# Two SwiGLU layers on one core: first gate and up products held in PSUM around the last norm, VectorE's order there written out, and the stream split for the projections out of SBUF

## The chip, the core and the metric

The kernel runs on one core of a Trainium2 chip. The core has a matrix engine (TensorE, PE in the rows), VectorE (DVE), ScalarE (ACT), GpSimd (POOL) and a queue engine (SyncE, SP) that issues most of the transfers between device memory and the on-chip memory SBUF. Matrix products are summed in PSUM, which the kernel uses as eight banks. The metric is the device time of one execution in microseconds (us); lower is better.

## What is computed

One inference step of a two-layer trunk on 1088 tokens (1024 of a prompt, 64 of eight sampled sequences) of width 1024. Layer 0 mixes by causal trailing means, layer 1 by dilated window attention; after each mixer comes a SwiGLU block, and between the layers one key/value and one query projection are made of the residual stream:

```python
def _rmsnorm(x, g):
    xf = x.astype(F32)
    y = xf * lax.rsqrt(jnp.mean(xf * xf, axis=-1, keepdims=True) + EPS)
    return (y * g.astype(F32)).astype(x.dtype)

def _swiglu(h, w_gate, w_up, w_down):
    return (jax.nn.silu(h @ w_gate) * (h @ w_up)) @ w_down
...
# layer 0:  x += PoolMix(RMSNorm(x));       x += SwiGLU(RMSNorm(x))
# then:     kv = RMSNorm(x) @ w_kv          (keys: per-head norm and rotary)
# layer 1:  x += DilatedAttn(RMSNorm(x));   x += SwiGLU(RMSNorm(x))
```

## The kernel before

**Precision.** Every f32 operand of a product is split in a high and a low part (`split`, L198 on ScalarE makes the high part, L199 on VectorE the low one), and every product is three matmuls (`mm3`, L202 to L204). A weight tile is split just before it is used.

**Layout.** The residual stream is `xall`, 128 partitions by 8 feature chunks by 1088 tokens. The tokens are handled as four quarters of 272 (`NB`), q0 to q3, or, for the projections, as nine tiles of 128 (the last of 64) in the order `TORD` = 5, 6, 7, 8, 0, ..., 4.

**SwiGLU.** Gate and up are computed by a scheme of seven block products for two-by-two blocks. The left factors are blocks of the weight or sums of them (`STEPS`: A11, A12, S2, S3, S1, A22, S4; the sums are made on VectorE, L423 to L428), the right factors are blocks or sums of the normed stream (`MATE`: B11, B21, T2, T3, T1, T4, B22), one tile of 128x1088 for each half g = 0, 1. B11 and B21 need quarters q0 and q1 only (`forms_one`). The five others need q2 and q3 too (`forms_two`, L269 to L279): half 0 needs q0 and q2, half 1 needs q1 and q3. All five are made from `xall` in place, so `xall` ends as scratch and its memory is given back; the stream itself has been stored to device memory (`spill`) and is loaded again for the down product. A unit of gate_up is 128 columns of the gate or the up weight: seven products for two halves of 12 matmuls each (168 matmuls). The output of the first product of a unit is copied out of PSUM by ScalarE into a tile `u` (L488); the tiles `u` lie in memory that `xall` held.

**The norm** of a quarter (`Norm.finish`): sums of squares over features by matmuls with a column of ones (L243), reciprocal square root on VectorE (L190 to L195), a transposition that spreads it over the partitions (L252), a copy on ScalarE (L254), and eight multiplications on VectorE (L257).

**Start of gate_up.** `EARLY = 2` gate/up pairs, four units, load their A11 and A12 blocks ahead (`load_early`) and run the products with B11 and B21 first, 192 matmuls, before the first product that needs a T form. Each engine executes its own instructions in order; where no manual order is set, a scheduler chooses that order when the program is built (before, GpSimd's order alone is manual in this part).

**Down.** `Down.run` goes through the steps A11, S1, S2, S4, S3, A12, A22, the first six over both halves (eight banks, 264 matmuls each), the last one half at a time. After S3 the quarters q2 and q3 of the stream are finished: VectorE adds the bank to a tile `du` (L630), GpSimd adds that twice into the stream (L631, L632), sixteen additions. `after(q)` is called when quarter q is done: it stores the quarter (layer 0) or writes output (layer 1). The weights of down come in tiles of 512 KB through a small pool of buffers.

**After down of layer 0** `split_stream` loads the nine tiles of the stream from device memory into `skt`, splits them into yh and yl, squares them on ScalarE, sums the squares per token (L721), and makes one matmul with ones per tile; from these sums comes the norm that the projections apply at their end. The weights of the projections are scaled by the norm's gain and split on ScalarE (L778) and VectorE (L779).

**PSUM** is divided by names: in gate_up and down all eight banks are "f" (`STR_PS`), elsewhere `FFN_PS` and `ATT_PS`.

## Time and profile before

| what | value |
|---|---|
| median of 3 runs | 3232.81 us (3223.08 to 3241.59) |
| the profiled execution | 3224.75 us |
| its span, first to last instruction | 3223.0 us |
| TensorE busy | 3056.5 us, 95% of the span |
| mean granted TensorE clock | 0.965 of full speed |
| layer 0: mixer; norm and forms; gate/up; down | to 136; to 180; to 632; to 881 us |
| projections; attention; output projection w_o | to 1790; to 2350; to 2458 us |
| layer 1: norm and forms; gate/up; down; last stores | to 2506; to 2955; to 3214; to 3223 us |

The busy share is a mean over stages. The stage borders are read from the timeline of the engines and are rounded. TensorE idles in a few places only, and nearly all of them lie where one stage ends and the next begins.

### The profile page before, as it was taken

The numbers are of one execution on the slowest core, as the hardware profiler recorded it, in microseconds if no ns is written. First come the engines' busy times: TensorE is split into PE (matmuls) and PEld (weight loads), VectorE is DVE, ScalarE is ACT, GpSimd is POOL, SyncE is SP. The second block draws the span as 40 slices with busy tenths as digits, with TensorE's granted clock in tenths as the row PEclk, the third lists the DMA queues.
The fourth block names the chain that finished last, engine by engine and source line by source line (L and its number), as shares of the span: only waits on it lengthen the run. The fifth ranks groups of instructions, "written<-read, shape, count | busy, mean of one in ns | idle before, by whom it ended". The sixth has DMA issues, their size and how long they took to land.

```text
span 3223.0 us, 56332 instructions
## 1 busy us (share of the span) xinstructions
PE 3056.5 (95%) x20467; PEld 2782.2 (86%) x20467; DVE 2315.0 (72%) x4669; ACT 1412.9 (44%) x4384; POOL 704.8 (22%) x829
## 2 busy tenths in 40 slices
PE   6599999999889999999999899999997899999998
PEld 6599999999877777777777788888897899999998
DVE  4676666667689999888893477777747666665675
ACT  4333322333466555243351577776723332232333
POOL 2313333255200000000000002222213233333551
PEclk8699999999999999999999799999998999999999
DMA  6336777788866776876965758686474267778876
GB/s 233 124 113 208 256 252 241 272 315 278 303 174 228 237 228 213 315 269 219 338 209 159 207 170 281 225 278 223 145 248 159 92 238 242 243 250 297 285 271 230
DMA packets 318106, 747.00 MB, mean 232 GB/s; under 512 B 38366, under 2 KB 140814, under 8 KB 315029
## 3 DMA queue, kind: packets, MB, share of 16 engines
q1 hardware_dynamic: 284103, 515.79, 49.3%
q0 software_dynamic: 5376, 174.60, 15.0%
q10 hardware_dynamic: 28350, 53.03, 4.5%
q8 instruction: 161, 2.64, 0.3%
q14 instruction: 116, 0.95, 0.1%
HBM read 629.57 MB, written 295.37 MB: 287 GB/s over the span
## 4 chain that ended last, share of the span: by engine, by line
PE 81%; DMA 7%; DVE 5%; issue 2%; POOL 2%; ACT 2%; SPq 0%; ACTq 0%; DVEq 0%; POOLq 0%
PE ps_f L202 12%; PE ps_f L204 12%; PE ps_f L203 12%; PE ps_s L1095 4%; PE ps_o L1128 4%; PE ps_s L202 3%; PE ps_s L203 3%; PE ps_s L204 3%; PE ps_a L202 2%; PE ps_a L204 2%; PE ps_a L203 2%; PE ps_p L203 2%; PE ps_p L202 2%; DMA wraw<-in_w_down 2%; PE ps_p L204 2%
## 5 line engine op out<-in xcount | busy, mean ns | idle before, releaser
L169 POOL DMA_DIRECT2D out_kv_sample<-in_cache_kv_w x168 | 83.8, 502 | 1466.1 <-PE ps_o L204 898.5
L202 PE MATMUL ps_f<-hf,wsplit 128*128 128x272 f32 x1232 | 342.4, 291 | 14.6 <-DVE du L630 5.5
L203 PE MATMUL ps_f<-hf,wsplit 128*128 128x272 f32 x1232 | 350.2, 289 | 0.5 <-DVE hf L199 0.5
L204 PE MATMUL ps_f<-hf,wsplit 128*128 128x272 f32 x1232 | 339.7, 290 | 6.2 <-DVE wsplit L199 6.2
L202 PEld LDWEIGHTS ps_f<-hf,wsplit 128*128 128x128 f32 x1232 | 229.9, 191 | 17.1 <-ACT wsplit L198 9.0
L199 DVE TENSOR_TENSOR wsplit<-wraw,wsplit 128x512 fp32r<-128x512 f32 (+1 forms) x250 | 189.1, 766 | 72.3 <-ACT wsplit L198 66.5
L198 ACT CAST wsplit<-wraw 128x512 fp32r<-128x512 f32 (+1 forms) x250 | 153.4, 633 | 196.8 <-DVE wsplit L199 76.4
L204 PEld LDWEIGHTS ps_f<-hf,wsplit 128*128 128x128 f32 x1232 | 228.0, 190 | 7.7 <-DVE wsplit L199 7.3
L203 PEld LDWEIGHTS ps_f<-hf,wsplit 128*128 128x128 f32 x1232 | 233.9, 190 | 0.7 <-DVE hf L199 0.7
L198 ACT CAST wsplit<-wsplit 128x512 fp32r<-128x512 f32 x176 | 108.6, 619 | 273.0 <-PE ps_f L204 272.2
L199 DVE TENSOR_TENSOR hf<-hraw,hf 128x544 fp32r<-128x544 f32 (+1 forms) x176 | 166.7, 955 | 83.6 <-ACT hf L198 83.5
L199 DVE TENSOR_TENSOR wsplit<-wsplit 128x512 fp32r<-128x512 f32 x176 | 155.0, 882 | 65.0 <-ACT wsplit L198 64.6
L198 ACT CAST hf<-hraw 128x544 fp32r<-128x544 f32 (+1 forms) x176 | 102.6, 590 | 174.6 <-PE ps_f L204 151.7
L1106 ACT ACTIVATE S<-S,ml 128x128 f32<-128x128 f32 (+1 forms) x384 | 169.1, 443 | 22.3 <-DVE ml L1101 21.7
L199 DVE TENSOR_TENSOR vl<-vc,vh 128x512 fp32r<-128x512 f32 x208 | 143.9, 715 | 47.6 <-ACT vh L198 46.9
L461 POOL TENSOR_TENSOR sg<-sg,ct 128x544 f32<-128x544 f32 x66 | 103.8, 1573 | 309.6 <-DVE ct L459 193.2
L747 DVE TENSOR_TENSOR spr<-skt,sqb 128x1024 f32<-128x1024 f32 x128 | 155.2, 1212 | 20.8 <-DMA sqb<-q 19.9
L748 DVE TENSOR_REDUCE sc<-spr 128x16 f32<-128x1024 f32 x128 | 154.4, 1206 | 1.0
L1128 PEld LDWEIGHTS ps_o<-wsplit,P 128*128 128x128 f32 x1120 | 143.7, 196 | 6.9 <-ACT U L1132 1.1
L1128 PE MATMUL ps_o<-wsplit,P 128*128 128x64 f32 x1120 | 148.0, 273 | 0.7 <-ACT U L1132 0.5
L198 ACT CAST vh<-vc 128x512 fp32r<-128x512 f32 x208 | 122.8, 617 | 58.6 <-DMA vc<-in_cache_kv_w 31.7
L1095 PE MATMUL ps_s<-akT,aqT 64*128 64x128 f32 x1120 | 142.5, 301 | 0.0
(439 smaller groups left out, 10254.5 us busy)
## 6 DMA issues: line engine op xcount, KB each, us to landing
sqb<-q SPq DMA_DIRECT2D x128, 512.0 KB
wraw<-in_w_down SPq DMA_DIRECT2D x104, 512.0 KB
vc<-in_cache_kv_w SPq DMA_DIRECT2D x208, 256.0 KB
skt<-in_cache_kv_w SPq DMA_DIRECT2D x96, 512.0 KB
wraw<-in_w_gate SPq DMA_DIRECT2D x48, 512.0 KB
wraw<-in_w_up SPq DMA_DIRECT2D x48, 512.0 KB
wraw<-in_w_kv SPq DMA_DIRECT2D x48, 512.0 KB
out_kv_sample<-in_cache_kv_w POOLq DMA_DIRECT2D x24, 960.0 KB, 7.1
```

Of the source, the lines that this page charges most:

```text
L169: c = bulk.dma_start(_raw(kv_s[b], (n * WIN[b] + r) * row, [[row, m], [1, row]]), _raw(caches[b], (n * WIN[b] + r + TS) * row, [[row, m], ...
L198: nc.scalar.copy(h, x)
L199: nc.vector.tensor_sub(l, x, h.bitcast(FT))
L202: nc.tensor.matmul(out, wh, xh, start=first, stop=False, **kw)
L203: nc.tensor.matmul(out, wh, xl, start=False, stop=False, **kw)
L204: mark[0] = nc.tensor.matmul(out, wl, xh, start=False, stop=last, **kw).ins
L461: nc.gpsimd.tensor_mul(s, s, t)
L747: nc.vector.tensor_mul(pr, kt, qb)
L748: nc.vector.tensor_reduce(sc[b][:, :, n * TS + t], pr.rearrange("p (h d) -> p h d", d=HD), axis=AX.X, op=OP.add)
L1095: nc.tensor.matmul(ps[hh][:, c:c + 128], self.qT[hs, jj, :], kt[hs, jj, :], start=True, stop=True)
L1106: nc.scalar.activation(subs[hh][:, e], subs[hh][:, e], AF.Exp, bias=self.ml[:, 0, h:h + 1], scale=-1.0, accum_out=self.ml[:, 1, h:h + 1])
L1128: nc.tensor.matmul(self.po[:, h % 8 * 64:h % 8 * 64 + 64], Ps[hh][:, c:c + 128], vv[:, h * 64:(h + 1) * 64], start=z == 0, stop=z == nb - 1)
```

## The change

It has four parts.

1. **Around the last norm of each layer.** One bank is taken from "f" and named "n" for the sums and the transposition of the last quarter's norm. Only two units are loaded ahead. Their eight products with B11 and B21 (12 matmuls each) are started with seven "f" banks and kept there; nothing is copied out until the forms are done (`drain`, L546). The sums of q3 stand ahead of the products, its transposition (`apply`) ahead of the eighth product, the forms behind it. VectorE's order is manual here; the forms are made half by half and form by form (`FORMS`: T2, B22, T1, T3, T4), with tiles of their own for each half.
2. **Layer 1.** w_o goes through the quarters as q0, q2, q1, q3 (`QORD`); the norms of q0, q2 and q1 run as `pending` pieces between the products of w_o, and the forms of half 0 are made there too.
3. **Stream split.** The tiles of the stream are split straight out of `xall`: tiles 5 to 8 inside down, when S3 has finished q2 and q3 (`after0`, with an "f" bank), tiles 0 to 4 at the start of the projections. The nine loads into `skt` go. The stores of x1 move from SyncE's queue to GpSimd's.
4. **Smaller.** The outputs of layer 1 are written in halves of 512 features, the first half of tiles 0 to 4 after A12; the scores of the sampled tokens multiply in place; the attention's output is split by quarters (`pieces`); gate_up has one copy group more.

```diff
-STR_PS = {"f": 8}
+STR_PS = {"f": 7, "n": 1}
+DOWN_PS = {"f": 8}
+QORD = (0, 2, 1, 3)
...
+            self.sums(q, tag)
+            self.apply(q, gain, tag)
+        def sums(self, q, tag):
...
+        def apply(self, q, gain, tag):
...
-    def forms_two(X):
...
+    def forms_sum(g):
+        y11, y12, y21, y22 = quarter(0, g), quarter(0, g + 2), quarter(1, g), quarter(1, g + 2)
+        nc.vector.tensor_sub(y12, y22, y12)
+        nc.vector.tensor_add(y11, y11, y12)
+        nc.gpsimd.tensor_sub(y21, y11, y21)
+
+    def forms_two(X, g, f):
+        y11, y12, y21, y22 = quarter(0, g), quarter(0, g + 2), quarter(1, g), quarter(1, g + 2)
+        split(*X[f, g], {"T2": y11, "T3": y12, "B22": y22, "T1": y22, "T4": y21}[f])
+        if f == "B22":
             nc.vector.tensor_sub(y22, y22, y11)
+    FORMS = ("T2", "B22", "T1", "T3", "T4")
...
-    EARLY = 2
...
-        for n in range(2 * EARLY):
-            load_early(n)
-        for j in range(7):
+        dve = tc.manual_schedule(engines={mybir.EngineType.DVE})
+        dve.__enter__()
+        load_early(0)
+        load_early(1)
+        step = iter(begin)
+        first = {}
+        def drain(n):
+            u = tiles(n)
+            for g in range(2):
+                nc.scalar.copy(u[:, g], first[n, "A11", g][:, :NB])
+            for g in range(2):
+                take(n, "B11", g, first[n, "A12", g][:, :NB], u[:, g], OP.add)
+        for n in range(2):
+            for f in ("A11", "A12"):
+                for g in range(2):
+                    if n and f == "A12" and g:
+                        for done in step:
+                            done()
+                        prep(0, "A11")
+                        pl = open_pool()
+                        drain(0)
+                    p = first[n, f, g] = bank("f")
+                    product(p, n, f, g, True, True)
+                    if n == 0 and f == "A11":
+                        next(step)()
+        drain(1)
+        dve.__exit__(None, None, None)
+        for j in range(1, 7):
             prep(0, STEPS[j])
-        for n in range(2 * EARLY):
-            one(n)
...
+    def begin(X, gain, norm, rest):
+        def sums():
+            norm.sums(3, "n")
+        def apply():
+            norm.apply(3, gain, "n")
+            forms_sum(1)
+        def forms():
+            for f in FORMS:
+                for g in rest:
+                    forms_two(X, g, f)
+        return sums, apply, forms
...
-            x = pl.tile([128, D], FT, name="skt", bufs=3).rearrange("p (k t) -> p k t", k=8)
-            for q in range(o // NB, (o + n - 1) // NB + 1):
-                lo, hi = max(o, q * NB), min(o + n, (q + 1) * NB)
-                sync.dma_start(x[:, :, lo - o:hi - o], x1[q][:, :, lo - q * NB:hi - q * NB])
+            x = xall[:, :, o:o + n]
...
+    def after0(q):
+        if q != "A12":
+            spill("x1", (q,), x1, bulk)
+        if q == 3:
+            split_stream(yp[0], TORD[:4], "f")
...
     def projections():
+        split_stream(y2, TORD[4:], "p")
...
-            split_stream(pl, TORD[:4])
             load(0)
-            split_stream(pl, TORD[4:])
...
-            for q in range(4):
+            for q in QORD:
...
+                        if m < 6 and pending:
+                            pending.pop(0)()
+                if m4:
                     spill("x2", (q,), x2)
-                    nq.finish(q, G_F1, "s")
-                    forms_one(X, q)
+                    if q < 3:
+                        pending += ending(q)
...
+    form_tiles_two(X, xb.enter_context(pool("xb1", side="left")))
+    forms_sum(0)
+    for f in FORMS:
+        forms_two(X, 0, f)
...
+    def after1(q):
+        if q == 3:
+            output((5, 6, 7, 8), 0)
+            output((5, 6, 7, 8), 1)
+        elif q == "A12":
+            output((0, 1, 2, 3, 4), 0)
...
```


What stands where, TensorE first: the norm of q2 (`ps_s`), the norm of q3 and the first products with B11 and B21 (`xB11h`, `xB21h`; the last row of a product ends its twelfth matmul). Before:

```order
L252 MATMUL ps_s<-ident,nrs 128x128 x2
L252 MATMUL ps_s<-ident,nrs 128x16
L243 MATMUL ps_s<-ones,wsplit 128x1 x2
L243 MATMUL ps_s<-ones,wsplit 16x1
L252 MATMUL ps_s<-ident,nrs 128x128 x2
L252 MATMUL ps_s<-ident,nrs 128x16
L202 MATMUL ps_f<-xB11h_84,wsplit 128x272
```

After the change, first where the products begin, then where the transposition of q3 stands:

```order
L269 MATMUL ps_s<-ident,nrs 128x128 x2
L269 MATMUL ps_s<-ident,nrs 128x16
L255 MATMUL ps_n<-ones,wsplit 128x1 x2
L255 MATMUL ps_n<-ones,wsplit 16x1
L204 MATMUL ps_f<-xB11h_84,wsplit 128x272
L205 MATMUL ps_f<-xB11l_85,wsplit 128x272
```

```order
L205 MATMUL ps_f<-xB21l_89,wsplit 128x272
L206 MATMUL ps_f<-xB21h_88,wsplit 128x272
L269 MATMUL ps_n<-ident,nrs 128x128 x2
L269 MATMUL ps_n<-ident,nrs 128x16
L204 MATMUL ps_f<-xB21h_90,wsplit 128x272
L205 MATMUL ps_f<-xB21l_91,wsplit 128x272
```

The sums of q3 went to a bank of their own, the transposition of q3 stands behind 84 matmuls of the early products (it stood ahead of all of them), and only one of the eight products is behind it.

VectorE at the end of S3 in down of layer 0: `du` is the last addition out of PSUM, `hf` and `wsplit` are the splits that the next products need. Before:

```order
L630 TENSOR_TENSOR du<-du,ps_f 128x272 x2
L199 TENSOR_TENSOR hf<-hraw,hf 128x544
L630 TENSOR_TENSOR du<-du,ps_f 128x272 x6
L199 TENSOR_TENSOR wsplit<-wraw,wsplit 128x512
L199 TENSOR_TENSOR hf<-hraw,hf 128x544
L199 TENSOR_TENSOR wsplit<-wraw,wsplit 128x512
```

After the change, from the row that follows `hf` there:

```order
L201 TENSOR_TENSOR yl_6453<-xall,yh_6452 128x1024
L790 TENSOR_REDUCE tsa<-wsplit 128x128
L201 TENSOR_TENSOR yl_6455<-xall,yh_6454 128x1024
L790 TENSOR_REDUCE tsa<-wsplit 128x128
L201 TENSOR_TENSOR yl_6457<-xall,yh_6456 128x1024
L201 TENSOR_TENSOR ys<-xall,ys 128x8x64
L790 TENSOR_REDUCE tsa<-wsplit 128x128
L201 TENSOR_TENSOR wsplit<-wraw,wsplit 128x512 x5
L790 TENSOR_REDUCE tsa<-wsplit 128x64
L201 TENSOR_TENSOR wsplit<-wraw,wsplit 128x512
L192 TENSOR_SCALAR tms<-ps_f 128x4
L201 TENSOR_TENSOR wsplit<-wraw,wsplit 128x512
```

Four tiles of the stream (`yl`, `ys`), their four sums of squares (`tsa`) and the reading of the sums' bank (`tms<-ps_f`) came between; of the splits of the next weights, five stand ahead of the fourth sum and one ahead of `tms`.

VectorE at the end of down of layer 0: the last subtractions out of PSUM, then the projections. `yl` are tiles of the stream, `wsplit<-wraw,gcol` the weights of the first unit of the projections. Before (these weights stand some rows ahead of this piece):

```order
L199 TENSOR_TENSOR yl_9331<-skt,yh_9330 128x1024
L721 TENSOR_REDUCE tsa<-skt 128x128
L199 TENSOR_TENSOR yl_9333<-skt,yh_9332 128x1024
L199 TENSOR_TENSOR yl_9335<-skt,yh_9334 128x1024
L721 TENSOR_REDUCE tsa<-skt 128x128
```

After the change:

```order
L683 TENSOR_TENSOR xall<-xall,ps_f 128x272 x4
L790 TENSOR_REDUCE tsa<-wsplit 128x128
L781 MEMSET ps_p 128x9
L201 TENSOR_TENSOR yl_9405<-xall,yh_9404 128x1024
L201 TENSOR_TENSOR yl_9407<-xall,yh_9406 128x1024
L790 TENSOR_REDUCE tsa<-wsplit 128x128
L201 TENSOR_TENSOR yl_9409<-xall,yh_9408 128x1024
L201 TENSOR_TENSOR yl_9411<-xall,yh_9410 128x1024
L790 TENSOR_REDUCE tsa<-wsplit 128x128
L201 TENSOR_TENSOR yl_9413<-xall,yh_9412 128x1024
L865 SCALAR_TENSOR_TENSOR wsplit<-wraw,gcol,wsplit 128x512 x6
L790 TENSOR_REDUCE tsa<-wsplit 128x128
```

Five tiles of the stream and their sums stand now ahead of the first weights of the projections.

## Rows read from the trace of the kernel before

**Rows 1.** The page, busy time of the engines.
```profile
PE 3056.5 (95%) x20467; PEld 2782.2 (86%) x20467; DVE 2315.0 (72%) x4669; ACT 1412.9 (44%) x4384; POOL 704.8 (22%) x829
```

**Rows 2.** TensorE's waits, 130 to 200 us: total, times, longest us.
```profile
PE ps_s L252 <- DVE nrs L195: 16.9, 2, 15.2
PE ps_f L202 <- ACT u L488: 6.5, 1, 6.5
```

**Rows 3.** Table by windows: busy us (instructions) per engine, granted clock, DMA share, GB/s.
```profile
180.00:185.00 5.00, 4.91 (x23) 4.91 (x24) 4.70 (x8) 4.36 (x11) 0.00 (x0) 0.54 0.28 82
...
240.00:300.00 60.00, 60.00 (x481) 60.00 (x480) 41.07 (x65) 17.64 (x33) 19.72 (x17) 1.00 0.57 195
```

**Rows 4.** VectorE's timeline, 138 to 182 us: start, us, line, operation, count.
```profile
140.45 3.39 DVE L257 SCALAR_TENSOR_TENSOR xall<-xall,gcol,wsplit 128x272 f32<-128x272 f32 x8 [1.48 <-ACT wsplit L254]
...
148.86 3.48 DVE L279 TENSOR_TENSOR xall<-xall 128x1088 f32<-128x1088 f32 x1
...
157.63 3.39 DVE L257 SCALAR_TENSOR_TENSOR xall<-xall,gcol,wsplit 128x272 f32<-128x272 f32 x8 [1.48 <-ACT wsplit L254]
160.93 3.69 DVE L199 TENSOR_TENSOR wsplit<-wraw,wsplit 128x512 fp32r<-128x512 f32 x6
...
177.14 1.27 DVE L199 TENSOR_TENSOR xT4l<-xall,xT4h 128x1088 fp32r<-128x1088 f32 x1
178.35 1.27 DVE L199 TENSOR_TENSOR xT1l<-xall,xT1h 128x1088 fp32r<-128x1088 f32 x1
```

**Rows 5.** TensorE's waits, 2455 to 2520 us.
```profile
PE ps_s L252 <- DVE nrs L195: 16.8, 2, 15.2
PE ps_f L202 <- ACT u L488: 8.3, 1, 8.3
```

**Rows 6.** VectorE's timeline, 2455 to 2512 us.
```profile
2458.37 0.77 DVE L1283 TENSOR_TENSOR xall<-xall,ps_a 128x272 f32<-128x272 f32 x2
...
2503.27 1.29 DVE L199 TENSOR_TENSOR xT4l<-xall,xT4h 128x1088 fp32r<-128x1088 f32 x1 [3.50 <-ACT xT4h L198]
2504.48 1.28 DVE L199 TENSOR_TENSOR xT1l<-xall,xT1h 128x1088 fp32r<-128x1088 f32 x1
```

**Rows 7.** Chain that ended last, 770 to 830 us: start, us, what.
```profile
777.75 4.05 DMA wraw<-in_w_down
...
801.32 8.07 DMA wraw<-in_w_down
```

**Rows 8.** GpSimd's timeline, 780 to 832 us.
```profile
811.80 0.76 POOL L631 TENSOR_TENSOR xall<-xall,du 128x272 f32<-128x272 f32 x1 [13.56 <-DVE du L630]
812.52 1.24 POOL L632 TENSOR_TENSOR xall<-xall,du 128x272 f32<-128x272 f32 x1
...
827.99 1.22 POOL L632 TENSOR_TENSOR xall<-xall,du 128x272 f32<-128x272 f32 x1
```

**Rows 9.** Table by windows, start of step A12 in down of layer 0.
```profile
810.00:815.00 5.00, 3.15 (x14) 3.18 (x15) 4.94 (x11) 2.69 (x6) 3.20 (x4) 0.50 0.76 228
815.00:820.00 5.00, 5.00 (x38) 5.00 (x38) 4.41 (x5) 1.17 (x2) 5.00 (x6) 0.90 0.43 117
```

**Rows 10.** TensorE's waits, 878 to 905 us.
```profile
PE ps_o L202 <- ACT yh L198: 14.1, 1, 14.1
```

**Rows 11.** ScalarE's timeline, 878 to 905 us.
```profile
894.49 1.04 ACT L198 CAST yh<-skt 128x1024 fp32r<-128x1024 f32 x1 [6.12 <-DMA skt<-x]
```

**Rows 12.** VectorE's timeline, 878 to 905 us.
```profile
877.80 0.75 DVE L779 SCALAR_TENSOR_TENSOR wsplit<-wraw,gcol,wsplit 128x512 fp32r<-128x512 f32 x1
...
897.91 1.99 DVE L721 TENSOR_REDUCE tsa<-skt 128x128 f32<-128x1024 f32 x1 [1.12 <-ACT skt L720]
```

**Rows 13.** Table by windows, start of the projections.
```profile
895.00:900.00 5.00, 4.38 (x10) 3.01 (x11) 3.32 (x3) 3.47 (x4) 0.00 (x0) 0.50 1.04 305
900.00:905.00 5.00, 5.00 (x21) 4.08 (x20) 4.97 (x5) 3.83 (x8) 0.00 (x0) 0.86 0.60 184
```

**Rows 14.** Table by windows, end of the kernel.
```profile
3220.00:3223.00 3.00, 0.00 (x0) 0.00 (x0) 0.00 (x0) 0.00 (x0) 0.00 (x0) 0.50 0.50 199
```

More of the change, by code (lines that the diff above doesn't have):

```diff
@@ L204, in mm3, with pieces @@
         mark[0] = nc.tensor.matmul(out, wl, xh, start=False, stop=last, **kw).ins
+    def pieces(o, n):
+        for q in range(o // NB, (o + n - 1) // NB + 1):
+            lo, hi = max(o, q * NB), min(o + n, (q + 1) * NB)
+            yield q, lo - q * NB, hi - q * NB, lo - o, hi - o
     def blk(a, q):
@@ L394, in split_form, with gate_up @@
         return h, l
-    def gate_up(layer, X, pl, hd, ncopy, then):
+    def gate_up(layer, X, open_pool, hd, ncopy, begin, then):
+        pl = None
         wsrc = {"g": I["w_gate"][layer], "u": I["w_up"][layer]}
@@ L477, in store, with tiles @@
             sync.dma_start(hd[f, c], s.rearrange("p g t -> p (g t)"))
-        def one(n):
+        def tiles(n):
             c, nm = UNITS[n]
@@ L636, in run @@
                             nc.vector.tensor_sub(x21, x21, p)
-                if fa == "S3":
+                if fa == "A12":
+                    after("A12")
+                elif fa == "S3":
                     after(2)
@@ L641, in run, with swiglu @@
                     after(half)
-    def swiglu(layer, X, xa, xs, xb, after):
+    def swiglu(layer, X, xa, xr, xs, xb, begin, mid, after):
         nonlocal xall
@@ L653, in then @@
             d.append(Down(layer, hp.enter_context(pool("dh")), hd))
-        with pool("g1", side="left") as pl:
-            gate_up(layer, X, pl, hd, 3, then)
+        gate_up(layer, X, open_pool, hd, 3, begin, then)
+        gp.close()
         xb.close()
-        with pool("dk", side="left") as kp, pool("xd", side="left") as xd:
-            xall = xd.tile([128, 8, T], FT, name="xall")
+        psum_shares(DOWN_PS)
+        mid()
+        xall = xr.enter_context(pool("xd", side="left")).tile([128, 8, T], FT, name="xall")
+        with pool("dk", side="left") as kp:
             for q in (0, 2, 1, 3):
@@ L1259, in tile_yoco_step, with ending, apply @@
     x2, norms = {}, {}
+    def ending(q):
+        def apply():
+            norms[q].apply(q, G_F1, "s")
+            if q < 2:
+                forms_one(X, q)
+        return lambda: norms[q].sums(q, "s"), apply
+    pending = []
     with pool("wox", side="left") as wox:
@@ L1315, in tile_yoco_step, with output @@
-    swiglu(1, X, xa, x2, xb, output)
+    form_tiles_two(X, xb.enter_context(pool("xb1", side="left")))
+    forms_sum(0)
+    for f in FORMS:
+        forms_two(X, 0, f)
+    def output(part, h2):
+        for i in part:
+            o, n = TILES[i]
+            p = bank("f")
+            for j in range(4):
+                nc.tensor.transpose(p[:n, j * 128:(j + 1) * 128], xall[:, h2 * 4 + j, o:o + n], ident)
+            y = wide_tile()[:, :512]
+            (nc.scalar.copy if i % 2 else nc.vector.tensor_copy)(y[:n], p[:n])
+            dst = O["y_prompt"][0, o:o + n] if i < 8 else O["y_sample"].rearrange("n t d -> (n t) d")
+            sync.dma_start(dst[:, h2 * 512:(h2 + 1) * 512], y[:n])
```

127 lines of the change are left out of this document (56 added, 71 removed).

## The prediction

> **What bounds the kernel now.** I read the page first. TensorE is busy 3056.5 of 3223.0 us [rows 1], so what a change can save or cost lies in the 166 us in which it idles, and in the time that it runs at half clock after idling. The waits say where these are. At the last norm of layer 0 it waits 15.2 us for the reciprocal root of q3 and then 6.5 us for a copy into a tile `u` [rows 2]; layer 1 shows the same pair, longer by what 16.8 and 8.3 add [rows 5]. At the start of the projections it waits 14.1 us for the first tile of the stream [rows 10]. The table by windows gives the two prices of a matmul: 481 in 60 us at full clock, 0.125 us each, and 23 in 5 us just after an idle stretch, at a granted clock of 0.54, close to the lower of the two levels, 1.2 GHz [rows 3]. So each restart costs about (40 − 23) × 0.125 = 2.1 us beside the wait.
>
> At the norm the reader should see who is late. VectorE's timeline has no gap there: the scale of q2 from 140.45, forms, the scale of q3 from 157.63, weight splits, forms, the last one ending at 178.35 + 1.27 = 179.6 [rows 4]. The copy of `u` waits for that last form, since `u` lies where `xall` was, and TensorE resumes at about 180.1 (4.91 us busy in the window from 180 [rows 3]). It has then done 96 of the 192 early matmuls. The bound at this place is VectorE's work up to the last form, not TensorE's supply of products.
>
> **The change, part by part.**
>
> *Norm of layer 0.* Two units are loaded ahead, not four. TensorE can begin when VectorE has split the first weights, four splits at 3.69/6 = 0.61 us behind q2's scale, 144.5 for the first one [rows 4]. It holds seven products, 84 matmuls: 5 us at half clock for 23, then 61 × 0.125 = 7.6, so to 157.1. The transposition of q3 stands behind them. The scale of q3 therefore begins at about 158.6, a microsecond later than before, though the early products have used the wait. The eighth product begins only when its bank is copied out, and that copy still waits for the last form. Behind q3's scale (to 162.0) VectorE's order after the change has 13 small instructions (sums and splits of the weights of units 0 and 1) and 14 of 128x1088 (forms and splits of both halves) up to that form: 13 × 0.61 + 14 × 1.21 (the distance of two starts [rows 4]) = 24.9 us. Before it was 18.7 us, 160.9 to 179.6, since much of half 0 was done during the wait. A subtraction of GpSimd beside it stretches one of them from 1.28 to 3.48, 2.2 us more. So TensorE resumes at 187 to 189.5, with 84 matmuls done against 96 at 180.1: 7 to 9.4, plus 12 × 0.125 = 1.5. Bounds 8.5 and 11; I take **+10**.
>
> *Norm of layer 1.* Counted from the end of w_o's last addition, 2459.1, TensorE before resumes 47 us later, behind the last form's end at 2505.8; there VectorE has stood 3.50 us, waiting for a high part whose input GpSimd subtracts [rows 6]. After: five forms and splits of half 0 (6.0), the scale of q1 (3.4), four weight splits (2.4), three splits (3.6) bring VectorE to 15.4; the first products can start at 10 to 12, so 72 of them at the two prices end at 21 to 23; with the transposition and the copy the scale of q3 runs to 26.5 to 28.5; then 13 small and 8 large instructions, 17.6, and 2.2 for the subtraction beside them: 46.3 to 48.3. That is 0 to 1 us later than before, and 12 matmuls less are done (1.5); up to 2 more if the blocks of unit 1 land late. The work that moved under w_o is saved, but q3's chain is as long. Bounds +0.5 and +4.5; **+2**.
>
> *Split of tiles 5 to 8 inside down.* This is the largest term. Step A12 needs all eight "f" banks, and `split_stream` takes one of them for its sums. The bank comes free when `tms` has read the fourth sum. Until then TensorE can do seven banks of one chunk and, between the sums, little more: 63 + 24 = 87 matmuls. The stream's tiles wait for the last additions of GpSimd: 16 of them from 811.80 to 829.2, 1.09 us each; the first took 0.76, the next, beside VectorE, 1.24 [rows 8]. The 13th ends at 821.7 by 0.76 and at 826.0 by 1.09. I take 823, since VectorE will mostly stand still then. The Trainium skill (page SBUF — State Buffer, section Who interferes with whom) says that GpSimd and a VectorE instruction with two SBUF inputs exclude each other for a whole instruction. By that rule 821.7 would be right and the term 1 us smaller; the rows of 0.76 and 1.24 agree with it.
>
> From there: 1.0 for the copy on ScalarE [rows 11], then on VectorE three splits at 1.2, a small one at 0.6 and three sums over features at 2.0 [rows 12], 10.2; one weight split, 0.6, which frees a buffer for w_down. The split ahead of `tms` needs the 512 KB that are loaded into this buffer: 4.05 to 8.07 us [rows 7], then 0.65 and 0.6 for its split, and the reading: 12 + 6 + 1.5 behind 823 is 842.5; bounds 839 and 848. Before, TensorE had done 14 + 38 matmuls by 820 [rows 9] and went on at 0.125, so 232 by 842.5; 232 − 87 = 145, or 18 us, and 2 for the restart. What delayed `du` to 811.8 before [rows 8], weight splits that waited for w_down [rows 7], still stands ahead of it. The stores of x1, moved to GpSimd's queue, stand behind its additions, so nothing that this stall waits for is behind them. Bounds +15 and +26; **+20**.
>
> *Start of the projections.* Before, the first weights were split while the last products ran, and TensorE waited for the stream: stores, then a load, 14.1 us. Now tiles 5 to 8 are there, but VectorE has five splits at 1.2 and three sums at 2.0 ahead of the first low weights, 12.7 behind down's end, then six weight splits at 0.75 at most [rows 12], a sum, and two more weight splits whose 512 KB can be loaded only when the first buffer is free, 14.1 behind the end; 4 to 8 us [rows 7] bring it to 18 to 22. So the first unit's 46 matmuls end 21 to 25 us behind the end, at 902 to 906 (the wait of 14.1 us began at 881.5, since the first matmul behind it ran from 895.6, the end of the copy that started at 894.49 [rows 11]). Before, 10 had run by 900, 21 more by 905 [rows 13], and at 0.21 us each the 46th ended near 908. That saves 2 to 6, and the restart that now comes later gives 2 back: **−2**, bounds −5 and +2. The load was hidden badly before; what follows it now is VectorE.
>
> *The rest.* The last stores take 3 us without TensorE [rows 14]; with halves **−1** (0 to −3). Fewer early loads, the copy group more, in-place scores and split quarters change no wait on this path: 0, covered by TensorE's matmuls of gate_up and attention; uncovered, a VectorE instruction more costs 0.6.
>
> Sum: +10 + 2 + 20 − 2 − 1 = **+29 on the profiled 3224.75 (span 3223.0), 3254**. The median of the runs is 8 us above the profiled one, so the same sum there gives 3262. I forecast 3256, between them. The bounds added up are +16 and +43.5; +16 on the profiled time and +43.5 on the median, 3241 to 3276, are the forecast's own range.
>
> **The rivals.** (1) *The change works as it is drawn*: early products in the 15.2 us wait save some 10 in each layer, the split in down costs nothing, the projections start at once (−12), the stores −2: 3191. For it: TensorE really stands idle there, and 84 matmuls fit. Against it: the release is VectorE's last form, and it comes later. It decides if the last form of layer 0 ends before 170. (2) *Not slower, by the norm*: if the copy of `u` is released as soon as a bank is full and not by the last form (its place in memory being elsewhere), the T products follow each form as it comes; −10 in each layer instead of +12 in both, with the 20 in down and the −3 of the rest: 3222. For it: the wait's row names ScalarE's copy and not what it waited for; against: in layer 0 TensorE resumed 0.5 us behind the last form. It decides if the drain starts before 175. (3) *Not slower, by the bank*: if the tiles of the stream come so early, or the eighth bank is needed so late, that the stall in down costs only 5 us, 12 + 5 − 3 = +14: 3239. It would need `tms` before 826; the additions alone end at 822 or later. (4) *Worse*: after the stall the w_down buffers run behind, each transfer at 8 us, and down stalls again; 10 to 20 us more than the sum, 3264 to 3284.
>
> **How the numbers follow.** Within 0.5% (16 us) a measurement of this kernel can hardly be told from no change. The forecast 0.50, rival 1 0.13, rival 2 0.13, rival 3 0.14, rival 4 0.10. Slower by over 0.5%: the first and the fourth, 0.60; within: rivals 2 and 3, 0.27; faster: 0.13. The range, 3220 to 3280, reaches from rival 2 into rival 4 and leaves out rival 1 and the far end of rival 4.
>
> **What would show it.** In the new trace the transposition of q3 should stand at 157, the last form end at 187 to 189, and TensorE wait for the copy of `u` until then; in down of layer 0 TensorE should have a hole of some 20 us behind S3 that ends with `tms`, VectorE meanwhile showing sums of 2.0 us; at the projections it should run in small pieces for 20 us. I am wrong if the eighth bank of A12 does not wait for `tms`, or if the last form comes before 180.

## The result and the profile after

The changed kernel takes **3324.43 us** (median of 4, 3318.88 to 3341.2) where the kernel before takes 3233.68 us (median of 4): 1.029 times as long, 95% interval 1.0244 to 1.0339. Slower was the forecast, 3256 us, but the time is 44 us above the upper end of the range. The profiled execution of the changed kernel took 3318.88 us, with a span of 3316.8 us, 93.8 us longer than before.

First the page's engine totals, which answer to [rows 1]:

```profile
PE 3064.4 (92%) x20467; PEld 2796.6 (84%) x20467; DVE 2319.9 (70%) x4680; ACT 1408.5 (42%) x4387; POOL 714.2 (22%) x835
```

The engines have hardly more work: TensorE 8 us, VectorE 5, GpSimd 9. The other 85.9 of the 93.8 us are idle time of TensorE. Where they are comes from the timelines of TensorE, read at five matmuls: the first product of down in layer 0, the last one, the first product of attention, the first of w_o, and the last of gate_up in layer 1 that reads B22. Durations of the stages in us, of the profiled execution of each kernel (worked out, not a view, and good to about half a us; the kernels e1 to e18 are the experiments below):

| kernel | norm, gate_up | down 0 | projections | attention | w_o to B22 | rest | span |
|---|---|---|---|---|---|---|---|
| before | 633.4 | 248.1 | 909.8 | 555.1 | 613.8 | 262.8 | 3223.0 |
| changed | 648.4 | 262.0 | **983.1** | 547.4 | 613.2 | 262.7 | 3316.8 |
| e1 | 647.2 | 262.8 | 890.8 | 561.3 | 614.8 | 265.8 | 3242.7 |
| e2 | 634.5 | 252.2 | **1006.1** | 555.7 | 622.5 | 262.8 | 3333.8 |
| e3 | 648.0 | 254.6 | 895.3 | 551.2 | 614.5 | 266.3 | 3229.9 |
| e4 | 645.8 | 257.5 | 890.2 | 581.7 | 628.6 | 262.1 | 3265.9 |
| e5 | 648.0 | 251.1 | 877.4 | 563.0 | 617.1 | 265.8 | 3222.4 |
| e6 | 637.1 | 252.0 | 882.4 | 553.2 | 611.0 | 260.8 | 3196.5 |
| e8 | 634.0 | 251.9 | 884.9 | 561.0 | 611.9 | 260.3 | 3204.0 |
| e9 | 645.1 | 259.1 | 893.7 | 533.8 | 609.5 | 266.1 | 3207.3 |
| e12 | 648.9 | 266.1 | 949.6 | 551.7 | 614.4 | 266.2 | 3296.9 |
| e13 | 647.2 | 263.1 | 987.3 | 662.5 | 625.7 | 266.4 | 3452.2 |
| e14 | 647.9 | 263.2 | 977.2 | 567.4 | 615.3 | 262.5 | 3333.5 |
| e16 | 648.2 | 259.3 | 898.8 | 561.2 | 615.2 | 262.6 | 3245.3 |
| e18 | 644.5 | 253.0 | 877.7 | 567.0 | 613.2 | 262.4 | 3217.8 |

Norm and gate_up are 15.0 us longer, down 13.9, the projections 73.3; attention is 7.7 shorter. The projections are the stage that the prediction had made 2 us shorter. In them TensorE stands 90.4 us in the changed kernel, 24.9 before, and 18.4 in e1.

**The projections.** TensorE's waits there, changed kernel, 900 to 1880 us (total, times, longest):

```profile
PE ps_a L204 <- DVE xn L918: 18.2, 3, 12.0
PE ps_o L204 <- DVE xn L918: 16.8, 1, 16.8
PE ps_p L204 <- DVE xn L918: 9.8, 2, 6.3
PE ps_s L204 <- DVE a L195: 8.7, 2, 8.3
PE ps_p L204 <- DVE a L196: 6.3, 1, 6.3
PE ps_p L890 <- DVE a L195: 4.6, 1, 4.6
PE ps_p L791 <- DVE tsa L790: 4.0, 2, 3.7
```

A matmul wants a PSUM bank, and the bank is still held by a tile whose per-head norm VectorE has not finished (`xn`, `a`; `tsa` is the stream's split). Table by windows (busy us and instructions per engine, granted clock, DMA share, GB/s), 50 us of the changed kernel:

```profile
1250.00:1300.00 50.00, 33.17 (x134) 26.05 (x133) 49.67 (x98) 17.64 (x124) 0.00 (x0) 0.83 0.90 305
```

The same 50 us of the kernel before:

```profile
1250.00:1300.00 50.00, 50.00 (x216) 39.76 (x216) 47.45 (x112) 27.51 (x165) 0.00 (x0) 1.00 0.70 228
```

VectorE is nearly full in both; what differs is what it does. Its groups by line, 1000 to 1400 us (count, busy us, mean ns), in the changed kernel:

```profile
L830 DVE TENSOR_TENSOR sqb<-skt,sqb 128x1024 f32<-128x1024 f32 x83 | 101.0, 1218 | 5.5 <-DMA sqb<-q 5.4
L831 DVE TENSOR_REDUCE sc<-sqb 128x16 f32<-128x1024 f32 x83 | 100.4, 1215 | 0.0
```

and in the kernel before:

```profile
L748 DVE TENSOR_REDUCE sc<-spr 128x16 f32<-128x1024 f32 x62 | 74.7, 1204 | 0.4
L747 DVE TENSOR_TENSOR spr<-skt,sqb 128x1024 f32<-128x1024 f32 x61 | 73.8, 1211 | 8.7 <-DMA sqb<-q 8.4
```

A score product costs 1.22 us as before (1.21), but 83 stand in these 400 us where 61 stood: 22 products and 21 sums more, (101.0 + 100.4) − (73.8 + 74.7) = 52.9 us of VectorE taken from the per-head norms. VectorE's timeline at the longest wait (changed kernel, from 1272 us):

```profile
1273.02 0.70 DVE L918 TENSOR_TENSOR xn<-low,rs 64x512 f32<-64x512 f32 x1
1273.62 2.35 DVE L831 TENSOR_REDUCE sc<-sqb 128x16 f32<-128x1024 f32 x2
1276.31 1.23 DVE L830 TENSOR_TENSOR sqb<-skt,sqb 128x1024 f32<-128x1024 f32 x1 [0.33 <-DMA sqb<-q]
...
1279.06 1.16 DVE L831 TENSOR_REDUCE sc<-sqb 128x16 f32<-128x1024 f32 x1
...
1280.78 1.21 DVE L830 TENSOR_TENSOR sqb<-skt,sqb 128x1024 f32<-128x1024 f32 x1
...
1282.59 1.21 DVE L830 TENSOR_TENSOR sqb<-skt,sqb 128x1024 f32<-128x1024 f32 x1
1283.72 0.68 DVE L918 TENSOR_TENSOR xn<-ps_o,rs 128x512 f32<-128x512 f32 x1
```

and TensorE's row behind it:

```profile
1284.55 0.76 PE L204 MATMUL ps_o<-wsplit,yh 128*128 128x512 f32 x1 [16.83 <-DVE xn L918]
```

Between two `xn` (10.7 us from start to start) VectorE makes six score instructions of 1.2 us, in an order that the scheduler chose when the program was built. In that order 72 of the 128 scores stand ahead of the 54th normed tile, where before it was 39. (Counted here and below are the tiles that VectorE norms straight out of a PSUM bank, `xn<-ps`.)

**The last norm, layer 0** (answers to [rows 2, 4]): TensorE's waits in the changed kernel, 130 to 200 us:

```profile
PE ps_f L204 <- ACT u L546: 33.2, 1, 33.2
PE ps_s L269 <- DVE nrs L197: 1.6, 1, 1.6
```

GpSimd's timeline there, the subtraction of the last forms, for half 0 and for half 1:

```profile
151.18 2.54 POOL L287 TENSOR_TENSOR xall<-xall 128x1088 f32<-128x1088 f32 x1 [11.97 <-DVE nms L192]
164.39 13.08 POOL L287 TENSOR_TENSOR xall<-xall 128x1088 f32<-128x1088 f32 x1 [10.67 <-DVE xall L286]
```

VectorE's timeline, the scale of q3, the wait that follows from the second subtraction, and the last form:

```profile
156.71 3.39 DVE L274 SCALAR_TENSOR_TENSOR xall<-xall,gcol,wsplit 128x272 f32<-128x272 f32 x8 [1.37 <-ACT wsplit L271]
...
179.15 1.29 DVE L201 TENSOR_TENSOR wsplit<-wsplit 128x512 fp32r<-128x512 f32 x2 [4.02 <-ACT wsplit L200]
...
186.43 2.49 DVE L201 TENSOR_TENSOR xT4l<-xall,xT4h 128x1088 fp32r<-128x1088 f32 x2
```

ScalarE's timeline shows why VectorE waited there (the weight's high part stands in ScalarE's order behind `xT4h`, and that waited for GpSimd's subtraction), and what releases the copy of `u`, the last form:

```profile
177.50 1.10 ACT L200 CAST xT4h<-xall 128x1088 fp32r<-128x1088 f32 x1 [11.67 <-POOL xall L287]
...
188.99 1.26 ACT L546 COPY u<-ps_f 128x272 f32<-128x272 f32 x4 [6.21 <-DVE xT4l L201]
```

The wait of 15.2 us is gone, and one of 33.2 stands in its place. It ends behind the last form, at 186.43 + 2.49 = 188.9, where that was 179.6 before. From there on TensorE does every matmul of gate_up 10.9 us later than before (the 200th and the last alike). At the first product of down, where it did not stop before, it then waits again, for a bank that VectorE reads (waits of 190 to 650 us):

```profile
PE ps_f L204 <- DVE ct L475: 3.9, 1, 3.9
```

In layer 1 (answers to [rows 5]) the waits of 2455 to 2680 us are led by

```profile
PE ps_f L204 <- ACT u L546: 24.5, 1, 24.5
```

**Down of layer 0** (answers to [rows 8, 9]): GpSimd's timeline of the changed kernel, its first and thirteenth addition:

```profile
824.75 0.77 POOL L678 TENSOR_TENSOR xall<-xall,du 128x272 f32<-128x272 f32 x1 [6.63 <-DVE du L677]
...
834.56 0.76 POOL L678 TENSOR_TENSOR xall<-xall,du 128x272 f32<-128x272 f32 x1
```

VectorE's timeline, the reading of the sums:

```profile
851.51 0.16 DVE L192 TENSOR_SCALAR tms<-ps_f 128x4 f32<-128x4 f32 x1
```

TensorE's timeline right behind it:

```profile
851.72 0.59 PE L204 MATMUL ps_f<-hf,wsplit 128*128 128x272 f32 x1 [1.12 <-DVE tms L192]
```

Two windows of the stall. In the first TensorE is nearly idle, in the second it runs 12 matmuls at a granted clock of 0.50:

```profile
835.00:840.00 5.00, 0.28 (x2) 0.28 (x2) 3.57 (x3) 4.65 (x5) 5.00 (x6) 0.93 0.02 10
840.00:845.00 5.00, 2.62 (x12) 2.54 (x13) 5.00 (x5) 4.79 (x9) 0.18 (x1) 0.50 1.00 353
```

Counted by steps of 264 matmuls, A12, the step in which the split lies, takes 34.8 us before and 50.2 after. S3 ahead of it, with the wait for `du` at its end, takes 38.5 us before; after the change that wait is gone and S3 takes 32.9.

### The profile page after: what moved, and what is told of

It reads as the page before. It is cut to its first block, busy times and chain, and to the rows that moved or that the text cites. A ratio compares the mean times of both kernels' runs of the same rounds, so it can differ in the third digit from the quotient of the medians.

```text
span 3316.8 us, 56397 instructions
## 1 busy us (share of the span) xinstructions
PE 3064.4 (92%) x20467; PEld 2796.6 (84%) x20467; DVE 2319.9 (70%) x4680; ACT 1408.5 (42%) x4387; POOL 714.2 (22%) x835
## 5 line engine op out<-in xcount | busy, mean ns | idle before, releaser
L201 DVE TENSOR_TENSOR hf<-hraw,hf 128x544 fp32r<-128x544 f32 (+1 forms) x176 | 167.6, 963 | 93.8 <-ACT hf L200 91.6
L830 DVE TENSOR_TENSOR sqb<-skt,sqb 128x1024 f32<-128x1024 f32 x128 | 155.8, 1218 | 13.6 <-DMA sqb<-q 13.5
L204 PE MATMUL ps_f<-xB21h,wsplit 128*128 128x272 f32 x352 | 103.7, 295 | 57.7 <-ACT u L546 57.7
L831 DVE TENSOR_REDUCE sc<-sqb 128x16 f32<-128x1024 f32 x128 | 154.9, 1216 | 0.3
```

The costliest lines, as they stand in the source:

```text
L201: nc.vector.tensor_sub(l, x, h.bitcast(FT))
L204: nc.tensor.matmul(out, wh, xh, start=first, stop=False, **kw)
L830: nc.vector.tensor_mul(qb, kt, qb)
L831: nc.vector.tensor_reduce(sc[b][:, :, n * TS + t], qb.rearrange("p (h d) -> p h d", d=HD), axis=AX.X, op=OP.add)
```

## The experiments

A ratio is that of the times to the kernel before, with its 95% interval in brackets. The theory is that the scores in place, the smallest-looking edit of the change, let the scheduler place the scores of the sampled tokens too early on VectorE in the projections. The first rival is that the later first product (norm and bank) or the split in down costs the time; the second that the write in place costs by itself.

**e1: the changed kernel with a product tile of its own.**

```diff
-            nc.vector.tensor_mul(qb, kt, qb)
-            nc.vector.tensor_reduce(sc[b][..., n * TS + t], qb.rearrange(...), ...)
+            pr = pl.tile([128, D], FT, name="spr", bufs=1)
+            nc.vector.tensor_mul(pr, kt, qb)
+            nc.vector.tensor_reduce(sc[b][..., n * TS + t], pr.rearrange(...), ...)
```

> The changed kernel with one thing undone: the scores of the sampled tokens multiply into a tile of their own again (one buffer), not in place. Theory: in place, up to three products can stand between multiplication and sum, so the scheduler packs the scores denser into VectorE's order (72 of 128 scores ahead of the 54th normed tile of the projections, 39 in the kernel before), and TensorE then waits for banks that VectorE reads late. Undone, the projections take 982.9 - 73 = about 910 us again and the run 3243 to 3255. Rival: the stream split at the start of the projections, the pool of its own for the keys or the new places of the y tiles delay VectorE; then the run stays above 3300.

3247.89 us (median of 10), ratio 1.004 (1.0021 to 1.0059). The projections fall by 92.3 us to 890.8, 19 below what was expected, the other stages stay within 14 us. 40 scores stand ahead of the 54th normed tile. This one edit carries the loss of the projections.

**e2: the kernel before with the scores in place**, the reverse of that edit and nothing else.

> The kernel before with one thing done: the scores multiply in place. Theory: the projections (first matmul 895.6 to the first attention product 1791.3) get some 60 to 75 us longer, the run 3285 to 3300, and the waits of TensorE name VectorE's xn. Rival (the in-place form costs nothing by itself): 3225 as before.

3335.59 us (one run). The projections grow by 96.3 us, more than the 60 to 75 expected, without any other part of the change; 73 scores stand ahead of the 54th normed tile. So nothing else in the change is needed for the loss.

**e3: e1 with tiles 5 to 8 split at the projections' start.**

```diff
-        if q == 3:
-            split_stream(yp[0], TORD[:4], "f")
...
+        split_stream(yp[0], TORD[:4], "p")
         split_stream(y2, TORD[4:], "p")
```

> As e1, and tiles 5 to 8 are split at the start of the projections too, not inside down. Theory (the bank that the sums hold stalls A12): down of layer 0 takes 248 us as before and not 262; VectorE then has 11 us more ahead of the first weights, and the projections start 9 to 12 us later: the run within 4 us of e1. Rival (the stall in down comes from late w_down buffers, not from the bank): down stays at 258 or more, and the run is 8 to 12 us longer than e1.

3231.95 us (one run). Down takes 254.6 us against 262.8 in e1, where 248 was expected; its step A12 alone goes from 50.0 to 34.7, as before the change, while the wait for `du` is back. The projections, which now hold the split, take 895.3 against 890.8. The run is shorter than expected, but attention, which the edit does not touch, gives 10 us of that.

**e4: e1 with the sums' matmuls of tiles 5 to 8 moved to the projections**, so that down's A12 has all eight banks; splits and sums over features stay in down.

> As e1, but the sums of squares of tiles 5 to 8 stay in SBUF during down; their matmuls with ones and the norm's root come after down, so no bank is taken in down. Theory (the bank): TensorE goes on through A12, down takes 248 to 251 us, the run is 10 to 14 us below e1. Rival (VectorE's 12 us of splits and sums delay the weights of A12 all the same): the gain is under 4 us.

3264.98 us (median of 5), ratio 1.0092 (1.0063 to 1.0121). Down takes 257.5 us, 5.3 less than e1, and that lies in A12, 44.8 us against 50.0: that much is the bank. The theory had given it all of the stall, 248 to 251 us; the other 10 us of A12 stay without the bank. TensorE's longest wait of 800 to 925 us is now for a weight split, which stands in ScalarE's order behind the splits of the stream:

```profile
PE ps_f L204 <- ACT wsplit L200: 8.5, 1, 8.5
```

The run is longer all the same, by attention (+20.4) and w_o (+13.8), in which the edit changes nothing. As a time of the whole it tells nothing of the split.

**e5: e3 with all nine stream tiles in one pool on the right side of SBUF.** In the windows of e1 TensorE does 219 to 220 matmuls in 50 us of the projections, before 216; in e1 tiles 0 to 4 lie on the right, before none.

```diff
-        yp.append(y_tiles(ystack.enter_context(pool("y1", side="left")), TORD[:4]))
+        pass
-    y2 = y_tiles(ystack.enter_context(pool("y2")), TORD[4:])
+    y2 = y_tiles(ystack.enter_context(pool("y2")), TORD)
```

> The kernel of e3 with all nine normed stream tiles in one pool on the right side of SBUF; in e3 tiles 5 to 8 lay on the left side. If the place of a tile sets the spacing of the products that hold it, the products of tiles 5 to 8 go from 0.2333 to 0.2266 us each, which over 4 of 9 tiles of some 885 us is 10 to 12 us: projections 880 to 885 us, span 3217 to 3221 us, run 3220 us. Rival, the spacing hangs on something else that differs between the tiles (their order, what runs beside them): projections stay at 895 us and the run at 3232 us.

3222.81 us (median of 8), ratio 0.9964 (0.9948 to 0.9979). The projections take 877.4 us, 17.9 less than in e3, 6 more than the place was to give.

**e6: the kernel before with the stream split out of SBUF at the projections' start and the nine tiles on the right**; norm, gate_up, down and scores as before.

> The kernel before, whole, with two things of the change alone: the stream is split out of SBUF at the start of the projections, and the nine tiles lie on the right side. The last norm, gate and up, down and the score products are as before. If the norm with its bank is what lengthens gate and up by 14 us and the front of down by some 6, the stretch up to the first down product goes back from 648 to 633 us, down to 248 to 250 us, and the projections to 880 to 890 us: run 3198 to 3208 us, faster than the kernel before by 0.8 to 1.1%. Rival, the stretch is longer for the stream's tile that stays in SBUF through down (both kernels of this pair have it): 643 us and 255 us, run 3220 us.

3207.21 us (median of 6), ratio 0.9911 (0.988 to 0.9942): faster than both kernels, by under 1% against the kernel before. Norm and gate_up take 637.1 us (633 was expected, 643 by the rival), 10.9 less than in e5, which has the change's norm. TensorE's waits at the last norm are those of before, 15.2 and 7.3:

```profile
PE ps_s L252 <- DVE nrs L195: 16.9, 2, 15.2
PE ps_f L202 <- ACT u L488: 7.3, 1, 7.3
```

**e8: the kernel before with the pool of the nine tiles on the right side, alone.**

```diff
-    ypool = ystack.enter_context(pool("y", side="left"))
...
     sc = {b: scpool.tile([128, H, ST], FT, name=f"sc{b}") for b in (2, 1)}
+    ypool = ystack.enter_context(pool("y"))
```

> The kernel before with one edit: the pool of the nine normed stream tiles is opened on the right side of SBUF, where it was on the left. If the place sets the spacing of the products (0.2333 us on the left, 0.2266 on the right), the projections shrink by 2.9% of some 880 us, 23 to 26 us: 884 to 888 us, run 3206 to 3212 us. Rival, e6 was faster by the split out of SBUF at the projections' start, not by the place: projections 908 us, run 3234 us.

3216.74 us (median of 10), ratio 0.9945 (0.9925 to 0.9966). The projections fall from 909.8 to 884.9 us, as expected; the run is 5 us above its forecast. A move of tiles from one side of SBUF to the other is worth 25 us in this stage, of which some 20 show in the median of the whole (3236.55 us for the kernel before beside it). The intervals of e6 and e8 overlap, so these two are not told apart.

**e12 and e13: the changed kernel with two buffers, and with one, for the sample queries** (`name="sqb", bufs=3` to 2 and 1).

> The changed kernel, in-place score products kept, with two buffers in place of three for the sample queries; the scheduler then places 51 scores ahead of the 54th normed tile, where the changed kernel has 72 and the kernel before 39. Theory, the loss in the projections is that scores stand too early on VectorE: it shrinks with the lead, 12 of 33 of the 73 to 92 us, so projections 910 to 945 us and a run of 3260 to 3285 us. Rival, the in-place write itself costs (the load of the next query waits for the reduction): with one buffer fewer it waits more, projections 985 us or longer, run 3325 us or more.

> The same with one buffer: 31 scores ahead of the 54th normed tile, 84 of 128 ahead of the 90th. Theory of the early scores: nothing left of the loss in the middle of the projections, 885 to 900 us up to the last product, and what is lost is behind it, where some 40 scores are left and attention waits for them: run 3240 to 3290 us. Rival of the in-place write: every load then waits for a multiplication and a reduction, projections 1000 us or longer, run 3340 us or more.

3298.87 us and 3454.04 us (one run each). e12's projections, 949.6 us, lie 5 us above what the theory gave and 35 below the rival's; its run is 14 us above the theory's. e13 went against its theory: with the scores late, the projections are still 987.3 us, and attention 662.5; the run is where the rival put it. VectorE's waits show why. The load of the next query in e12, 1000 to 1750 us (total, times, longest):

```profile
DVE sqb L830 <- DMA sqb<-q: 64.3, 41, 6.0
```

The same wait in e13, 1000 to 1900 us:

```profile
DVE sqb L830 <- DMA sqb<-q: 230.9, 84, 11.9
```

VectorE stands in its order for the load of the next query, which can start only when the buffer is read; the weight splits behind it come late (in e13 TensorE's longest group of waits, 21.6 us in four pieces, is on `wsplit`). So buffers are no clean measure of the order. Two runs separate them:

**e14: two product tiles and two query buffers, nothing in place; e16: one product tile and two query buffers.** Both are e1 with `bufs` changed.

> The changed kernel with the product in a tile of its own again, but with two product tiles and two buffers for the sample queries. Nothing is written in place, and the scheduler places 64 scores ahead of the 54th normed tile (72 in the changed kernel, 40 in e1). Theory of the early scores: projections 940 to 975 us in place of e1's 891, run 3295 to 3325 us. Rival, the write in place costs, not the order: projections 885 to 895 us, run 3240 to 3250 us.

> The kernel of e1 with two buffers for the sample queries in place of three: one product tile, 40 scores ahead of the 54th normed tile, as in e1. It tells what two query buffers cost by themselves, which e12 and the run with two product tiles share. Theory of the early scores: nothing or little, projections 889 to 905 us, run 3240 to 3260 us. Rival, two buffers make VectorE wait for the loads and that is the loss of e12: projections 930 us or longer, run 3285 us or more.

e14 takes 3335.59 us, e16 3247.2 us (one run each). e14 is 2 us over the upper end of what the theory gave for the projections, and its run 11 us. With the same two query buffers, 64 early scores give projections of 977.2 us and 40 give 898.8. Nothing is written in place in either, so the loss comes without the write; the two buffers by themselves cost 8 us (890.8 to 898.8). In e14 TensorE waits for the per-head norm as in the changed kernel; the first row of its waits, 910 to 1880 us:

```profile
PE ps_s L204 <- DVE xn L919: 13.5, 2, 10.9
```

The first row of e16 that names the per-head norm:

```profile
PE ps_o L204 <- DVE xn L919: 1.2, 1, 1.2
```

**e9 and e18: the subtraction of the last forms (L287) on VectorE**, in e1 and in e5.

```diff
-        nc.gpsimd.tensor_sub(y21, y11, y21)
+        nc.vector.tensor_sub(y21, y11, y21)
```

> The kernel of e1 with the subtraction of the last forms (y21 from y11) on VectorE in place of GpSimd, in both layers. If that subtraction, 13.1 us long on GpSimd beside VectorE, holds the end of the forms, PE's wait at the last bank of the first products falls from 33.2 to 29 to 31 us and the stretch up to the first down product from 647 to 643 to 645 us, run 3244 us. Rival, VectorE is full there and only gets longer by the two subtractions: PE waits 34 to 36 us, run 3250 us.

> The kernel of e5 (all tiles on the right, split at the projections' start, product tile of its own) with the last forms' subtraction on VectorE, the edit of e9. In e9 the stretch up to the first down product fell by 2.1 us and down by 3.7, where the whole run fell by 35: the rest is an attention stage of 534 us in place of 561 and 5 us in w_o, where the edit does nothing. If only the first two belong to the subtraction, gate and up take 645 to 646 us, attention 545 to 565 us, and the run 3213 to 3220 us, faster than e5 by 3 to 9 us. Rival, the subtraction shortens the later stages too: attention 535 us, run 3180 to 3192 us.

e9 takes 3209.18 us (one run), e18 3220.63 us (median of 4, ratio 0.9929, 0.9901 to 0.9957). In both TensorE's wait at the norm falls to 30.3 us, and the stretch to the first down product by 2.1 and 3.5 us:

```profile
PE ps_f L204 <- ACT u L546: 30.3, 1, 30.3
```

Of the 35.4 us by which e9's span is shorter than e1's, 27.5 lie in attention, and e18, with the same edit, has there 567.0 us. So the subtraction does not shorten attention, and e9's time is no time of the edit. The intervals of e18 and e5 overlap: over the whole the edit is not seen.

## Why the prediction was wrong, step by step

- **The rest, "in-place scores ... change no wait on this path: 0".** This step failed, and it is the miss. The cover named for it was TensorE's matmuls of gate_up and attention, and the price 0.6 us for a VectorE instruction more. But the scores stand in the projections, and no instruction was added: a score product takes 1.22 us as before, and its place in VectorE's order changed. One product tile had held the scores apart: a multiplication could not be placed before the sum that read the product ahead of it. Without it the scheduler placed 72 scores where it had placed 39, and TensorE waited for banks. Leaving this edit out gives 92.3 us back (e1), and it alone costs 96.3 (e2). That an early order does it without any write in place is shown by e14 and e16. Why the scheduler prefers the score to the norm of a tile stays open.
- **Norm of layer 0, +10.** Right: TensorE is 10.9 us later through all of gate_up. The transposition of q3 stands at 155.7 (157 was said), the last form ends at 188.9 (187 to 189), and the copy of `u` waits for it, which settles rival 2. In part that is luck. The subtraction was priced at 2.2 us and took 13.08, and VectorE then stood 4.02 us for a high part from ScalarE, which had stood for the subtraction; but q3's scale had begun at 156.7, 1.9 us ahead of what was said. Taking the subtraction from GpSimd gave 2.1 and 3.5 us back.
- **From gate_up to down: no term.** The wait of 3.9 us at the first product of down was not foreseen. The eleven kernels with the new norm wait 3.5 to 4.0 us there, the four with the norm of before (before, e2, e6, e8) not at all. PSUM is divided anew at this place (`STR_PS`, then `DOWN_PS`); whether that is the cause was not tried. With it the stretch to the first product of down took 647.7 us in the mean of the nine kernels with this norm and GpSimd's subtraction, and 634.8 in the four: +13.
- **Norm of layer 1, +2.** The stretch from w_o through gate_up took 613.2 us against 613.8. It took 609 to 629 us over the kernels, so +2 cannot be told from 0.
- **Split in down, +20.** The mechanism came as told, the size did not. VectorE's `tms` at 851.5 releases the bank, and 0.2 us later TensorE goes on, with 84 matmuls of A12 done (87 was said). The thirteenth addition ends 10.6 us behind the first start (11.2 was said), so they did run at 0.76 mostly. But from the start of A12 to the release it took 25.6 us where 30.7 was said (811.8 to 842.5), since VectorE's weight splits in it ran without the wait for w_down that was set in. So A12 is 15.4 us longer, at the lower bound of the term (49.8 to 50.4 us in the seven kernels with the split and the bank, 34.3 to 35.6 in the seven without). Of that e4 puts 5 on the bank; the other 10 stay when the bank is free and go only when the split leaves down (e3): they are the stream's splits and sums, which stand ahead of those of the next weights. And what was said to stand ahead of `du` did not: S3 takes 32.9 us in every kernel with the split, with no wait behind it, and 37.0 to 41.2 in those without; why was not traced. Down as a whole takes 262.2 us in the mean of the seven with, and 251.8 in the seven without (before, e2, e3, e5, e6, e8, e18): **+10**, not 20.
- **Start of the projections, −2.** Right, and a little more than said. Leaving out the matmuls of the sums, the 46th matmul behind down's end ends 24.2 us behind it (21 to 25 was said), and 28.3 before.
- **End, −1.** 262.7 us against 262.8: too small to be told.
- **The sum** on this profile, with the projections and attention left aside: 15.0 + 13.9 − 0.6 − 0.1 = +28, where 10 + 2 + 20 − 1 = +31 was said of these places. That agrees in part by chance, since a wait of 4 us was left out and down was put 6 to 10 too high. The projections, where −2 was said, are three quarters of the loss. Part of the loss is even hidden: without it, in e1, the projections are 19.0 us shorter than before, with tiles 0 to 4 on the right side.

Rival 4 (buffers of w_down behind) did not come: A22, the step behind A12, took 34.1 us, and 34.8 before; none of the rivals holds the mechanism that decided. The fastest version, e6, keeps from the change only the split out of SBUF and puts all nine tiles on the right side.

## What to carry to other kernels

Where a scheduler orders an engine, a buffer shared in turn is also what holds its users apart: before a tile is taken away, compare the order of that engine over the whole stage, not only where the change was aimed. Cost an edit at nothing only when the engine that runs it has slack in its own stage; VectorE was busy 47.45 of 50 us in the projections of before, which the prediction left out. And when one execution gains far more than its edit can reach, ask which stage gained.

## What was not expected of the hardware

**The side of SBUF on which a product's tile lies sets its spacing.** Groups of matmuls in the projections (count, busy us, mean ns), in the kernel before:

```profile
L204 PE MATMUL ps_s<-wsplit,yl 128*128 128x512 f32 x280 | 110.6, 395 | 0.0
```

and in e8, which differs in the side alone:

```profile
L204 PE MATMUL ps_s<-wsplit,yl 128*128 128x512 f32 x288 | 112.0, 389 | 0.0
```

In a window in which TensorE never stops, 216 matmuls fit into 50 us before and 222 in e8:

```profile
1250.00:1300.00 50.00, 50.00 (x222) 40.91 (x221) 48.82 (x120) 27.35 (x164) 0.00 (x0) 1.00 0.71 230
```

That is 0.231 against 0.225 us each, over all shapes in the window. That it is the place of the tile, and not of something else that moved with it, shows inside one kernel: in e1, at a granted clock of 1.00, the matmuls of tiles 0 to 3, on the right, start 227 ns apart, those of 6 and 7, on the left, 234 ns. Before, all of these start 234 ns apart, in e5, e6, e8 and e18, with all tiles on the right, 227. What about the place does it (distance, bank, or the neighbour that is read at the same time) was not tried.

**GpSimd beside a busy VectorE.** The subtraction of two 128x1088 tiles on GpSimd took 2.54 us at 151.18 and 13.08 us at 164.39, where VectorE's instructions stand back to back. It ended at 177.5, 2.3 us after VectorE had come to its stop of 4.02 us at 175.1; so it got through about when VectorE stood still. The Trainium skill (page SBUF — State Buffer, section Who interferes with whom), cited ahead for the exclusion of the two engines, goes the same way; the factor of five was measured here.

**Attention starts at either clock.** At the change from the projections to attention TensorE waits, 10.0 us in the kernel before, 12.1 in e9, 5.4 and 5.9 in e6 and e8. Before, the granted clock was then 0.50, the lower level of 1.2 GHz, for two windows of 10 us in which TensorE hardly stopped (table by windows):

```profile
1790.00:1800.00 10.00, 8.04 (x62) 6.47 (x60) 4.36 (x31) 5.77 (x17) 0.00 (x0) 0.84 1.07 245
1800.00:1810.00 10.00, 10.00 (x44) 8.43 (x44) 3.65 (x30) 7.87 (x38) 0.00 (x0) 0.50 1.07 231
1810.00:1820.00 10.00, 9.95 (x43) 8.44 (x43) 2.61 (x15) 4.11 (x16) 0.00 (x0) 0.50 0.26 76
```

In e9, whose attention starts at 1797.9, it was 1.00 in the next window:

```profile
1790.00:1800.00 10.00, 6.11 (x44) 5.27 (x45) 2.74 (x7) 2.52 (x5) 0.00 (x0) 0.56 1.05 259
1800.00:1810.00 10.00, 9.85 (x82) 8.26 (x81) 7.15 (x55) 9.97 (x40) 0.00 (x0) 1.00 1.09 231
1810.00:1820.00 10.00, 9.23 (x76) 8.16 (x74) 4.77 (x18) 8.46 (x36) 0.00 (x0) 1.00 0.99 264
```

44 and 43 matmuls against 82 and 76. They are not all the same matmuls: before, TensorE had waited for a load (`wraw<-kvn`), in e9 for `aqT`, so the orders differ there. Attention, in which no kernel here changes a line but the split by quarters, took 534 to 582 us over the kernels other than e13, so the time of a whole kernel can be 20 us off to either side for a stage that its edit does not touch. With one trace for each kernel it is not shown whether that goes with the execution or with the order that was built; the five runs of e4 (3263.6 to 3280.2 us) all lie above the ten of e1 (3241.1 to 3255.7). What decides which clock is granted stays open.
